# A two-layer hybrid trunk: four low parts of weights made by GpSimd, other banks for one memory attention, two slots for a small state, and a new order

## The chip, the cores and the metric

The kernel runs on one core of a Trainium2 chip. A core has engines that run side by side, each with its own queue of instructions: TensorE (PE in the profile) for matmuls, VectorE (DVE), ScalarE (ACT), GpSimd (POOL), and SyncE (SP), which issues the transfers from HBM to SBUF. Every queue is worked off in order. The metric is the device time of one execution in microseconds (us). Three runs of the kernel before took 1055.48, 1057.3 and 1059.38 us, so the median is 1057.3.

## The reference

Two layers over 256 tokens of width 1024, each of them three residual steps with a layer norm:

```python
for i in range(DEPTH):
    x = layer_norm(ALPHA * x + 0.5 * swiglu(x, ffn1_w_gate[i], ffn1_w_up[i], ffn1_w_down[i]), ln_g[i, 0], ln_b[i, 0])
    if i % N_MIXERS == 0:
        proj = x @ rwkv_w_in[j]
        mix = rwkv7_mix(proj[..., :RWKV_SHIFT], ...)
        mq = proj[..., RWKV_SHIFT:]
    else:
        proj = x @ sb_w_in[j]
        mix = stick_breaking_mix(proj[..., :c], proj[..., c:2 * c], proj[..., 2 * c:3 * c])
        mq = proj[..., 3 * c:]
    heads = jnp.concatenate([mix, memory_attention(mq, mem_k, mem_v)], axis=-1)
    x = layer_norm(ALPHA * x + heads @ w_out[i], ln_g[i, 1], ln_b[i, 1])
    x = layer_norm(ALPHA * x + 0.5 * swiglu(x, ffn2_w_gate[i], ffn2_w_up[i], ffn2_w_down[i]), ln_g[i, 2], ln_b[i, 2])
```

`swiglu` is `(silu(x @ w_gate) * (x @ w_up)) @ w_down` with an inner width of 2816. `rwkv7_mix` is a delta-rule recurrence over 12 heads of 64; its decay, its gate and its learning rate come from a low-rank part of the projection. `memory_attention` is a softmax attention of 4 heads over 256 memory tokens. All weights are float32 and are used once: some 300 MB are read from HBM.

## The kernel before

**Precision.** A product of float32 accuracy is made from three matmuls on rounded operands (type float32r): high part of the weight times high part of the activation, low times high, high times low (`mm3`, L858). So each weight is loaded in pieces of 128 x 1024 (512 KB) into a `raw` buffer; ScalarE copies it, rounded, into a `hi` buffer; VectorE subtracts the two and writes the rest to a `lo` buffer. That is `piece` (L824 to L846). There are 11 raw, 9 hi and 8 lo buffers, which are used in turn. A raw buffer is free for the next load when its low part has been made. For some chunks of the FFNs (the table `WHOLE`) w_down is used in plain float32, straight from the raw buffer.

**Stages.** The 256 tokens are two halves of 128. The FFN's inner width is cut into 11 chunks of 256: gate and up into PSUM banks of the tag `gu` (two banks), SiLU and product on ScalarE and VectorE, then the down product into the accumulators `acc0` (half 0) and `acc1` (half 1), two banks each; a fourth tag, `tp`, holds two banks for transposes and small work. While one half goes through the mixer (`rwkv`, L1213, in layer 0, `stick`, L1688, in layer 1), whose chains of small steps leave TensorE idle, chunks of the other half's FFN are mixed into it. In layer 0 `memory_kv` makes the keys and values of the memory, and `mem_attention(0, ..., MEMTAG)` (L1118, called at L1889) attends for half 0 near the end of that half's recurrence; MEMTAG names the tag of its banks. `mixed_out` multiplies by w_out; it takes the four row blocks of w_out in the sequence of a tuple in `ORDERS`, which it gets by number: 0 or 1 for half 0 (the layer), 3 for half 1. In `rwkv` the low-rank state `zl` has one buffer for both halves (L1259).

**What sets the order.** The program is recorded first and ordered afterwards. Class `Plan` (L296) records each instruction; `order` (L516) places them engine by engine, with a price for each operation (`price`, L457), and picks among the ready ones by priority; `improve` (L723) takes the priorities from the table `URGENCY`, a packed list of one number for each instruction, and the same numbers set the sequence in which loads, high parts and low parts go through their buffers. `issue` then emits all of them from one line, so nearly every instruction of the profile is at L788. In the names of the trace hi_49r or raw_15r is a buffer, not a weight.

Of the kernel before, what the change touches and what calls it, by code (L numbers as in the profile page):

```python
# [133 lines left out]
CHUNK0 = 94.7  # L134
ROUNDS = 50
# [8 lines left out]
    '+ZY#j58=v>V*I{r2%is%@tbQy7@-!goQW}iC9yi^DCd8%d<fS%%T3nVF2)sp3RDlFlCxc2G=z(<3L$ri5OVg7@f~qiliM4fjxn29N)-wr|H&A0T6'
    'e`maxIS!Hwodn4QjbQ#z&tCVaAuP^ZZn2*f%+ZLXXDy+vpIAf2Iz8w@~+D;;1Nw=-RPzxaF-F8~+sJyy+nfNQw8|7!URg;W0T~>8uxOsntX3Cy%+'
    'lk8y;!a@BF})9_R}#yQW&c%+8&zYXhm!%poG%J+zIbgvLPu2=f)F~0Cvj9+~i<6o^pxLfUOIM4TEVyq^A1=RA3>q59r9_wA33I!I*iSxX4PYA^d+'
    'wbmFsO{cdex8G+*{5SXaf@DZO`!+Hup-7iax?FS5WdV2W6|9q{AKN1+J}(6jI-FIhd#J5BO?@8k~`e>>YwrM3aPNOcskBcrT<SK6nid&()wc4Jux'
    'ml7Q)}lVti21n>B|MxNqc4kHX8579lLZS^n#VFkNj6sl`s`IaAHKPNd^2rBmVXzj8iMzF@lL+8B4~rTZI(Q2ogeIt+{PX8<mx*1y~z<LhnU4^FRX'
    'DZcz6xGc1mkN<v)u|%5~v&iuSS=2mxD*UQncER@eIWbO3$5_krH%<wm@_f1d2WA(9(0>TLT5}8>9~uzCp*Lb2G&qET{oNz>#baaKB7dtEIm2IK7#'
    '`zn*Z*)+jO*rwaI@!MUn3s5p3)rN9<g^<^{%d7W98nujel0#M!0C2{#CO9^1fBR#;t{!zti#D+i(Z7<3EqF^cx|dfcS&6uDw1LhMZ5w?)v>hn6Kb'  # L150
    '$-S?;COn90zTTN%B!tEE*@mGCx6Py-Q-%?+OFcGfmi=&FT#<UKhOScfF>Vt7JV;m`;ch?MIkep?mV$W;TXj2Fe&VtGPF}{qS3c~YfoHSgWs=g-wZ'
    '^7Ro_u_=Yui{>Lx+QBWZ2u!2d+Mvn_<NP}UDFQ+#6L;Sc2y1GQ#F6OMU3l<!@70vJC%-CKB}h9-&;R*EdhJhDsTV7xbS6!aqK(seGtM-N%&;4T09'
    'oQ{K_FL?4n0&$JnBGD&$`i;|#qr?|n7;i8lO|j`v(CrVsSXeXcDSLR<B?AcpdAGZQCGfd8w+T0^h2uN%Vme$Ny0P3~>|JFKZu3D<1KJ0Gjx2bZVg'
    'A9}OGarin8BOR^PEQE5MV;nNqHH}lDuo{-b7ro&ji#{DQFdh5;7D5v>p3y%Q=H3-!Q*q^8mX6zZ(WZ7G%!2O{a<TIzJmlV_*SpY^=k(meUfT&zv-'
    ';sPI=Esr9MFemU#Vxy5T2?Z!dcj@lkmR&>@mZ>8F&j%O~ogm61zLsr}}aVT)q7b{N)H?Bd+|g2_C+HSMlU1{Cz@gf2TS3;MF}-L%4jN`oewDYhr9'
    'Gwtg^QOOM<RFB|uzW1~G8Ve|*-SXYnFnPgwQw@IJg>h-E>)T>pDZ^`42@X=^pjQ{*Egs*Y)KxZu@)^_T(N*&(&I>!G-dAuitcm7Mq9l28B**v&Q4'
    '^&pGtn{bTelbr>$BcL6`{NMqxWrnkLwL7wI<8o(xBf>9^!A>LFh`Hp*|WQTObwUwg7S-tf02_s;wubOEk^Jat7v^T{joX5;>&R;JpU<<ulm3vt^b'
    '*3w<-xEH|d{RF^-XwT&rkIkq}PPuKn-DxWQ|CXw52|T8Iw4qNh&E?>2o=QS6r_7}C4V9uV*07)$#5o-bnTrj~nQex|%1_IEM$UaF?^)b>{W*HUfD'
    'rS&z_Fnj?nv`>52Wx@GF^y~pV*vEb|JomYp?S;!?F!_k{T|=XDKN#a-d8#>5&0zWoxzB*pEIsrBeteBbDbX<<*Yg6)pGbw>xaKSSEpCz#E|#~3*3'
    'I`%2;1|fV|F#nhcDW?r{rK7h<gu+^96je<TY9?-nVv$uNd4~@AYl+DYjnn(s5smH{1WhuQ7Ip#fE&?MDg9PM(=p8jh>(C_a}ZXJc85Q_Y`jaPhaG'  # L160
    'w1=U_mg+2{jcWsQvXW>}+y_0A7-0RD6$jh*n8^;!q*VXiEt{V2%UmIv_S3aUV>}+;zSDtSGY-GhtO=<9Peq@?hZ-(_6xbz1(IjI&^X!yJQz%KezQ'
    'QzOxAQj%9o{rrTznS2w0zTRv!YKE5mxJT-^aee-4vtsBbYA<vej|TkuZQ@DM59J~?ppfypBT=l&*AgxmuQc33>W89uvk)GU%54ePFvIQWqSM#4PA'
    'qC>frdp@LCdnYg=P7++QVEd7Lq8Ovfj0OodbWdp7>=Xa7d{Y6wkT!=t_FT;=HJ&Gf5)ntdqVoUW<u9F3cX@G7p{fLqr(%k$QqQaFT)@b#1WUGM(u'
# [1763 lines left out]
```

## Time and profile before

| what | value |
|---|---|
| median of three runs | 1057.3 us (1055.48 to 1059.38) |
| the profiled execution | 1058.2 us |
| its span | 1056.4 us |
| mean granted clock of TensorE | 0.995 |
| read from HBM | 300.95 MB, 286 GB/s over the span |

The page gives each engine's busy time and its share of the span. A table by stages gives the busy time of each engine in a stretch, so that a stall in one stage isn't lost in the average. The granted clock is the share of TensorE's full speed that the chip allowed; at 0.50 a matmul takes twice as long. In rows of single instructions the first number is the start, the second the duration; what stands in brackets at the end is the engine's idle time before it and what ended it.

### The profile page before, as it was taken

How to read it: one execution, taken by the hardware profiler on the slowest of the kernel's cores; microseconds unless marked ns; L12 is line 12 of the kernel's file. 1: busy time of each engine (PE TensorE's matmuls, PEld its weight loads, DVE VectorE, ACT ScalarE, POOL GpSimd, SP SyncE). 2: the span in 40 equal slices, each digit the busy share in tenths (PEclk: the TensorE clock that was granted, in tenths of full speed). 3: DMA queues.
4: the chain of work that ended last, by engine and by line, in shares of the span. 5: the costliest groups of instructions: out<-in, count | busy, mean ns of one | idle time of the engine just before them, and what ended most of it. 6: DMA issues, size and time to landing. Idle time of an engine off the chain costs nothing.

```text
span 1056.4 us, 17846 instructions
## 1 busy us (share of the span) xinstructions
PE 1041.8 (99%) x6275; PEld 835.8 (79%) x6275; DVE 886.2 (84%) x1241; ACT 741.6 (70%) x1064; POOL 5.3 (0%) x20
## 2 busy tenths in 40 slices
PE   8999999999899999999999999999999999999997
PEld 7788888877788776688888888888778777888885
DVE  6776679999799998898799765569899999976688
ACT  6665558968679877667577555457987998765573
POOL 0000000000000000000000000000000000000000
PEclk9999999999899999999999999999999999999999
DMA  9998869879399788799999976768989989998792
GB/s 307 332 368 259 265 201 357 266 247 331 130 328 336 250 273 295 247 341 315 307 325 352 311 246 208 226 213 262 369 309 315 366 274 304 366 366 256 265 317 76
DMA packets 212684, 303.19 MB, mean 287 GB/s; under 512 B 13892, under 2 KB 159728, under 8 KB 212594
## 3 DMA queue, kind: packets, MB, share of 16 engines
q1 hardware_dynamic: 212050, 301.53, 85.2%
q8 instruction: 49, 0.80, 0.3%
q10 hardware_dynamic: 544, 0.52, 0.2%
q14 instruction: 41, 0.34, 0.1%
HBM read 300.95 MB, written 1.05 MB: 286 GB/s over the span
## 4 chain that ended last, share of the span: by engine, by line
PE 95%; DMA 2%; DVE 1%; ACT 1%; issue 0%; SPq 0%; DVEq 0%; ACTq 0%
PE ps_30r L788 28%; PE ps_29r L788 27%; PE ps_26r L788 8%; PE ps_3r L788 8%; PE ps_27r L788 8%; PE ps_25r L788 8%; PE ps_5r L788 3%; PE ps_6r L788 3%; DMA raw_9r<-in_ffn_w_down_dram 1%; DMA raw_18r<-in_ffn_w_up_dram 1%; DMA raw_48r<-in_ffn_w_up_dram 1%; DMA raw_12r<-in_ffn_w_up_dram 1%; DVE x L788 0%; DVE L_345r L788 0%; DVE lo_47r L788 0%
## 5 line engine op out<-in xcount | busy, mean ns | idle before, releaser
L788 PE MATMUL ps_30r<-hi_46r,xTh 128*128 128x512 f32 (+1 forms) x70 | 28.2, 403 | 0.0
L788 PE MATMUL ps_30r<-hi_46r,xTl 128*128 128x512 f32 (+1 forms) x70 | 26.9, 385 | 0.0
L788 PE MATMUL ps_30r<-lo_17r,xTh 128*128 128x512 f32 x68 | 26.5, 390 | 0.0
L788 PE MATMUL ps_29r<-lo_11r,xTh 128*128 128x512 f32 (+1 forms) x64 | 24.6, 385 | 0.8 <-DVE lo_11r L788 0.8
L788 PE MATMUL ps_30r<-lo_11r,xTh 128*128 128x512 f32 x64 | 25.0, 390 | 0.0
L788 PE MATMUL ps_30r<-hi_10r,xTh 128*128 128x512 f32 x60 | 24.5, 409 | 0.0
L788 PE MATMUL ps_30r<-lo_8r,xTh 128*128 128x512 f32 x62 | 24.2, 391 | 0.0
L788 PE MATMUL ps_30r<-hi_10r,xTl 128*128 128x512 f32 x60 | 23.5, 392 | 0.0
L788 PE MATMUL ps_30r<-lo_14r,xTh 128*128 128x512 f32 x60 | 23.4, 390 | 0.0
L788 PE MATMUL ps_29r<-hi_65r,xTh 128*128 128x512 f32 x56 | 22.8, 407 | 0.0
L788 PE MATMUL ps_29r<-lo_17r,xTh 128*128 128x512 f32 x58 | 22.6, 390 | 0.0
L788 PE MATMUL ps_29r<-lo_47r,xTh 128*128 128x512 f32 (+1 forms) x58 | 22.2, 383 | 0.0
L788 ACT ACTIVATE idle_2r<-ps_29r 128x256 f32<-128x256 f32 (+1 forms) x27 | 11.1, 412 | 15.8 <-PE ps_29r L788 15.2
L788 PE MATMUL ps_30r<-hi_7r,xTh 128*128 128x512 f32 (+1 forms) x56 | 21.9, 392 | 0.0
L788 PE MATMUL ps_29r<-hi_65r,xTl 128*128 128x512 f32 x56 | 21.9, 392 | 0.0
L788 ACT ACT_TABLE_LOAD x16 | 20.5, 1283 | 2.0 <-issue 1.7
L788 PE MATMUL ps_30r<-lo_41r,xTh 128*128 128x512 f32 x56 | 21.9, 390 | 0.0
L788 PE MATMUL ps_29r<-lo_14r,xTh 128*128 128x512 f32 x56 | 21.8, 390 | 0.0
L788 ACT ACTIVATE idle_1r<-ps_29r 128x256 f32<-128x256 f32 (+1 forms) x27 | 11.7, 432 | 14.3 <-PE ps_29r L788 14.3
L788 PE MATMUL ps_30r<-hi_7r,xTl 128*128 128x512 f32 (+1 forms) x56 | 21.4, 383 | 0.0
L788 PE MATMUL ps_30r<-hi_65r,xTh 128*128 128x512 f32 x52 | 21.4, 412 | 0.0
L788 ACT ACTIVATE idle_2r<-ps_30r 128x256 f32<-128x256 f32 (+1 forms) x30 | 12.9, 431 | 12.0 <-PE ps_30r L788 12.0
(2124 smaller groups left out, 3945.5 us busy)
## 6 DMA issues: line engine op xcount, KB each, us to landing
raw_9r<-in_ffn_w_down_dram SPq DMA_DIRECT2D x16, 512.0 KB, 6.7
raw_48r<-in_ffn_w_down_dram SPq DMA_DIRECT2D x16, 512.0 KB, 6.0
raw_12r<-in_ffn_w_down_dram SPq DMA_DIRECT2D x16, 512.0 KB, 6.2
raw_18r<-in_ffn_w_gate_dram SPq DMA_DIRECT2D x31, 256.0 KB, 5.0
raw_18r<-in_ffn_w_up_dram SPq DMA_DIRECT2D x31, 256.0 KB, 4.6
raw_15r<-in_ffn_w_down_dram SPq DMA_DIRECT2D x15, 512.0 KB, 5.8
raw_9r<-in_ffn_w_gate_dram SPq DMA_DIRECT2D x30, 256.0 KB, 5.9
raw_9r<-in_ffn_w_up_dram SPq DMA_DIRECT2D x30, 256.0 KB, 5.8
```

Source lines behind the costliest of these rows:

```text
L788: fn(*[at(x) for x in a], **{n: at(x) for n, x in k.items()})
```

## The change

Four things change, and with them the order of the whole program.

1. `POOLED` names four low parts; `piece` has GpSimd do the subtraction for these, and VectorE for all others as before.
2. `MEMTAG` is 'gu' instead of 'acc1': memory attention for half 0 of layer 0 uses the two banks of gate and up.
3. `FLAGS["zl2"]` is on: `zl` has two buffers, one for each half.
4. The third tuple of `ORDERS` is another, and `URGENCY` is a new table.

```diff
-MEMTAG = 'acc1'
+MEMTAG = 'gu'
...
-ORDERS = ((3, 1, 2, 0), (1, 0, 2, 3), (2, 0, 3, 1), (3, 0, 1, 2))
-FLAGS = dict(t1=False, bt=False, dc=False, out1=False, zl2=False, pb=False, xt=False, mn=False, tn=False, vn=False, sq=True)
+ORDERS = ((3, 1, 2, 0), (1, 0, 2, 3), (1, 0, 2, 3), (3, 0, 1, 2))
+FLAGS = dict(t1=False, bt=False, dc=False, out1=False, zl2=True, pb=False, xt=False, mn=False, tn=False, vn=False, sq=True)
...
+POOLED = ('lo_882', 'lo_977', 'lo_1793', 'lo_1834')
...
-    'c-l?edAN<`8#exXZJ`Vel1617LVQJ~5}C>rqRb-7EK`I`Wr$LSMCK;Slp#|pG*IS>qJdB(A{9}r`}cX?{X35L{bL_{ueF}%zOVbb&g(qSYpq4?jW'
...
+    '3gd$uY'
...
-            made.append(nc.vector.tensor_sub(lo[:, part], raw[:, part], hi[:, part].bitcast(F32)))
+            by = nc.gpsimd if lo.tensor.name in POOLED else nc.vector
+            made.append(by.tensor_sub(lo[:, part], raw[:, part], hi[:, part].bitcast(F32)))
```

TensorE has the same 5261 matmul instructions in both programs; on average a group of them stands three places from where it stood. Three places are shown.

GpSimd, from the last memset of Y (the second half's recurrence in layer 0) to the end. Before:

```order
L788 MEMSET Y_340r 128x32x4
L788 MEMSET Lm_333r 128x768
L788 MEMSET Lm_333r 128x12x16
L1923 UNCONDITIONAL_BRANCH
L1923 ISA
```

and with the change, where `ISA` in the second row is a reload of GpSimd's library, put there in front of its first arithmetic, and raw, hi and lo are a piece's three buffers:

```order
L792 MEMSET Y_340r 128x32x4
L792 ISA
L792 TENSOR_TENSOR lo_17r<-raw_15r,hi_7r 128x1024
L792 MEMSET Lm_333r 128x768
L792 MEMSET Lm_333r 128x12x16
L792 TENSOR_TENSOR lo_17r<-raw_42r,hi_49r 128x1024
L792 TENSOR_TENSOR lo_41r<-raw_42r,hi_62r 128x1024
L792 TENSOR_TENSOR lo_17r<-raw_42r,hi_49r 128x1024
L1928 UNCONDITIONAL_BRANCH
L1928 ISA
```

The first subtraction came in between the memset of Y and that of Lm, the other three behind. The pieces are one of ffn2_w_down and one of ffn2's gate and up in layer 0, one of w_out and one of sb_w_in in layer 1.

SyncE, the loads of gate and up in FFN 2 of layer 0 that come next after that first piece (each raw buffer takes one load of gate and one of up). Before, at place 276 of its queue:

```order
L788 DMA raw_67r<-in_ffn_w_gate_dram 128x2x256
L788 DMA raw_67r<-in_ffn_w_up_dram 128x2x256
L788 DMA raw_70r<-in_ffn_w_gate_dram 128x2x256
L788 DMA raw_70r<-in_ffn_w_up_dram 128x2x256
L788 DMA raw_64r<-in_ffn_w_gate_dram 128x2x256
L788 DMA raw_48r<-in_ffn_w_gate_dram 128x2x256
L788 DMA raw_18r<-in_ffn_w_gate_dram 128x2x256
```

and at the same place with the change, with ScalarE's high parts of these loads behind them:

```order
L792 DMA raw_93r<-in_ffn_w_gate_dram 128x2x256
L792 DMA raw_93r<-in_ffn_w_up_dram 128x2x256
L792 DMA raw_15r<-in_ffn_w_gate_dram 128x2x256
L792 DMA raw_15r<-in_ffn_w_up_dram 128x2x256
L792 DMA raw_9r<-in_ffn_w_gate_dram 128x2x256
L792 DMA raw_18r<-in_ffn_w_gate_dram 128x2x256
L792 DMA raw_64r<-in_ffn_w_gate_dram 128x2x256
L792 ACTIVATE hi_62r<-raw_15r 128x1024
L792 ACTIVATE hi_10r<-raw_9r 128x1024
L792 ACTIVATE hT_487r<-ps_5r 128x512
L792 ACTIVATE eT_611r<-ps_6r 128x512
L792 ACTIVATE hi_13r<-raw_18r 128x1024
```

The third and fourth loads go into raw_15r now, the buffer that GpSimd's first subtraction reads, and so wait for GpSimd. (hT and eT are the turned softmax tiles of half 1's memory attention.) The hi_13r of the last row is read by TensorE in the pair `ps_29r<-hi_13r,xTh` and `ps_29r<-lo_41r,xTh`, at places 1584 and 1585 of its queue; at 1585 and 1586 it had `ps_29r<-hi_13r,xTh` and `ps_29r<-lo_14r,xTh` before.

TensorE, the scores of half 0's memory attention in layer 0, between two groups of the recurrence (vn, Sk; S, qr). Before:

```order
L788 MATMUL ps_26r<-vn_314r,Sk_344r 64x64 x2
L788 MATMUL ps_25r<-vn_314r,Sk_344r 64x64 x2
L788 MATMUL ps_27r<-memKT,mq_331r 128x256
L788 MATMUL ps_3r<-memKT,mq_331r 128x256
L788 MATMUL ps_6r<-S_113r,qr_377r 64x64 x2
L788 MATMUL ps_5r<-S_113r,qr_377r 64x64 x2
```

and with the change:

```order
L792 MATMUL ps_25r<-vn_314r,Sk_344r 64x64 x2
L792 MATMUL ps_26r<-vn_314r,Sk_344r 64x64 x2
L792 MATMUL ps_30r<-memKT,mq_331r 128x256
L792 MATMUL ps_29r<-memKT,mq_331r 128x256
L792 MATMUL ps_5r<-S_113r,qr_377r 64x64 x2
L792 MATMUL ps_6r<-S_113r,qr_377r 64x64 x2
```

Both stand at places 1193 to 1200 of TensorE's queue; the banks moved (ps_27r and ps_3r to ps_30r and ps_29r, and ps_25r, ps_26r and ps_5r, ps_6r traded places), the sequence did not.

More of the change, by code (lines that the diff above doesn't have):

```diff
@@ L144 @@
[L144 to L163, printed above, removed]
@@ new lines @@
+    'RB4LiOk9`Qt^dq8xN6Z->5+Yk?Jc_)@$S1L7!B;se$!#4c4{ypK5ttuR_gM^4hDGB5yxaqn)NMC?XO+S;S$4>Y7?24X>*XeJfJ1jq2TN)Y4gG8@;'
+    'H{p6k~X`E^dUr=LjP_o}|sECXvxWUWu;imYe9HQR`+8!NJ_uWIGLs(!vAvpKHsdDVsmMFOv=7RX9%&eF3Cs+A^){A2HvrikQvW@>rrKk~V1+w39}'
+    '8dIw{)rAM?V>^+ecUS|jPh?%)Gl}>-ruO|roH_r^G9n9E|Lk$9_lL3udUbSzYD?;Ho;{aLP2X?Q_aP~@9XeCwJ$>+BtJ;CSeB=DhIlfpYkyPElL?'
+    '5mhDiZrd)!r1Wonmi3eBVK&CAC;VU9T+`@gA-^F^eIOqD<WztUA1{h$H*lrXpnmRKGL_$E>?QI2pJU9MHqz=L~7oRyFvVsXJZ4-Wt{as6lSdoxD)'
+    '>c}GJgA5mSriGGBb+VrgIoZ=#<2GTp~?#6X?o)OuyUo}5__D`pp_nskpJXCvAXR{CIN;I`zDMQM@gVbQ;#8B`7c6zesaqFq^0gjDU?OcamE>W$rU'
@@ new lines @@
+    '3G+;A?bWX+)UMSKBk@-CbAj)eQ~f!?-3bgSh-~NHw?+_ZEE(5cAfE=bF37p%9>`)RJ~V#zQc=E98)Tz>Xu-U;_T;gNv^?rJ=sS)u$u~Oxt^pSJw&'
+    '>mP|Z?6wND8{2D7gloO2u)q3qgiFW5RR@`bwJqKCt_zz;Zcth4I)*&?4OimdIgnw9=kL_6*;5IJ{Mwe$dRdtanMR%%Hff|gRt(S~^3Hucq0)&TAr'
+    '7ZNGN=YD@sz3N0=U#nKnDbj8OytuDAHHXNPIPiDR)bKeXd#F!Q)|ECMzHOriwM8=D5b3j7H4J_w+*Msx&yeWUVCWNkZl}5d{%-wd>irKQEo#G+qa'
+    'xYUiLA(D$l9Bx&IYqSRaLL^`n@iylb*uyIjZTvzso$4W~WtOftQ8bM8bNgexe3_z)Rs>hRoS)*Ura8+N-IpUx?K1D&hx5kGrU*MpN$6yMzFd{OCy'
+    '@@OS3ANZY(<L36Z_wYC6Hzr0mxuV#evpLVg{d*BoO)R(IJzpHvs$HLpu2Q)1Z{66;-X>t)PvTkQrxJ7RQxW+s`)womeqNr-qNg_$;;$gUv6s9^Yg'
@@ L291 @@
+    'm+8B`7`j<U_3D$^?JI&)CA_0tLW4Ra!#*L<Oe)2<3Y5!C0KDIYl6)U+rbMS7Xs$z6jmKD%hX%wX43OivIE_2LjC@cw+~mKCy|DfMT1^@+2k@B|9='
+    '3gd$uY'
 )
```

274 lines of the change are left out of this document (143 added, 131 removed).

## The prediction

> **What bounds the kernel now.** I read the page first: the busy shares and the chain that ended last.
>
> ```profile
> PE 1041.8 (99%) x6275; PEld 835.8 (79%) x6275; DVE 886.2 (84%) x1241; ACT 741.6 (70%) x1064; POOL 5.3 (0%) x20
> PE 95%; DMA 2%; DVE 1%; ACT 1%; issue 0%; SPq 0%; DVEq 0%; ACTq 0%
> ```
>
> TensorE is busy for 1041.8 of the 1056.4 us of the span and carries 95% of the chain. A change that leaves its matmuls alone can take at most 1056.4 − 1041.8 = 14.6 us, plus what a slow clock makes the busy time longer. So the second view is a table by stage: where TensorE is idle, and where its clock drops.
>
> ```profile
> 268.00:272.00 4.00, 3.47 (x136) 2.84 (x139) 2.90 (x7) 2.16 (x5) 0.00 (x0) 1.00 0.95 347
> 272.00:276.00 4.00, 2.00 (x57) 1.54 (x50) 3.49 (x8) 2.96 (x10) 0.67 (x3) 0.84 0.04 14
> 276.00:280.00 4.00, 3.77 (x100) 3.25 (x100) 1.27 (x4) 3.11 (x8) 0.00 (x0) 0.50 0.01 4
> 280.00:282.00 2.00, 1.58 (x9) 1.45 (x10) 1.90 (x6) 0.63 (x2) 0.00 (x0) 0.62 0.53 143
> 420.00:440.00 20.00, 19.43 (x181) 12.79 (x181) 17.20 (x33) 10.65 (x16) 0.00 (x0) 1.00 0.65 209
> 1048.50:1056.40 7.90, 0.00 (x0) 0.00 (x0) 4.83 (x14) 0.20 (x1) 0.00 (x0) 0.78 0.19 66
> ```
>
> In each row the length comes first, then busy time of PE, weight loads, DVE, ACT and POOL; the third number from the end is the granted clock. The last 7.9 us have no matmul at all: the last layer norm and the stores. Between 268 and 282 TensorE idles 0.53 + 2.00 + 0.23 + 0.42 = 3.2 us, and after the 2.00 us its clock is at 0.50. The three granted clocks 0.84, 0.50 and 0.62 amount to 0.16 × 4 + 0.50 × 4 + 0.38 × 2 = 3.4 us of lost clock, some 3 of them while there was work. This stall, where the delta-rule state of half 0 and the memory attention of half 0 meet, is worth 3.2 + 3 = about 6 us. The third view, what TensorE waited for, shows that little else is left:
>
> ```profile
> PE ps_6r L788 <- DVE L_345r L788: 1.8, 2, 1.2
> PE ps_29r L788 <- DVE lo_11r L788: 0.8, 1, 0.8
> PE ps_5r L788 <- DVE S_113r L788: 0.6, 1, 0.6
> PE ps_6r L788 <- ACT memKT L788: 0.5, 1, 0.5
> PE ps_26r L788 <- DVE lo_50r L788: 0.2, 1, 0.2
> ```
>
> Only two short waits in the whole run are for a low part of a weight (lo_11r at the start, lo_50r). VectorE is late with a low part nowhere else, even where it is nearly full:
>
> ```profile
> 320.00:340.00 20.00, 20.00 (x116) 17.19 (x116) 19.69 (x31) 19.89 (x39) 0.00 (x0) 1.00 1.04 353
> 780.00:800.00 20.00, 20.00 (x96) 14.33 (x95) 19.68 (x34) 14.47 (x20) 0.00 (x0) 1.00 0.84 277
> 800.00:820.00 20.00, 20.00 (x97) 16.63 (x96) 19.83 (x32) 15.73 (x19) 0.00 (x0) 1.00 0.93 323
> ```
>
> VectorE has 19.7 of 20 us there, TensorE 20.00 of 20. A lighter VectorE in these windows buys no time.
>
> **The change part by part.** The sum is made against the profiled execution: 1058.2 us, 1.8 us of it outside its span of 1056.4. The median of the runs shown is 1057.3, 0.9 lower.
>
> *Memory attention in the gate and up banks.* The scores and outputs of half 0 go to ps_30r and ps_29r instead of ps_27r and ps_3r. Around the stall the rows of TensorE, VectorE and ScalarE stand in the same sequence as before, only with banks and buffers swapped. The waits named above come from data (L_345r, S_113r, memKT), not from a bank of the memory attention. The gate and up matmuls that take the banks next stood behind it on TensorE already. Cost 0; if a bank were the cover, the gate of the next chunk could be held back by the output's last eviction, some 0.6 us.
>
> *Two slots for the low-rank state.* Half 1 could write its state before half 0 had read its own. Before, the tile's second writing began long after the first state's last use:
>
> ```profile
> L788 ACT ACTIVATE zl_315r<-ps_5r,vc x4: 352/364/368, 171.3 to 313.3; 128x128 f32<-128x128 f32 x4
> 268.12 0.33 PE L788 MATMUL ps_5r<-vn_314r,kn_313r 64*64 64x64 f32 x4
> ```
>
> The last reader of half 0 (the product with g_up) stands just ahead of the matmuls at 268.12, and half 1's last writing starts at 313.3. More than 40 us lie between. Cost 0.
>
> *The third tuple of ORDERS.* Half 0 uses the first two, half 1 the fourth; the third is read by no one. Cost 0.
>
> *The new order.* TensorE issues the same matmuls with as many changes of shape; most rows move by a few places. It can win back the small waits outside the stall: 0.57 us in 420 to 440, 0.2 for lo_50r, and as much again elsewhere, 1 to 2 us; it can lose as much. I take −0.5.
>
> *Four low parts on GpSimd.* Removed from VectorE are four subtractions, 4 × 1.22 = 4.9 us, in stages where it has slack enough for TensorE:
>
> ```profile
> 345.74 1.22 DVE L788 TENSOR_TENSOR lo_44r<-raw_67r,hi_10r 128x1024 fp32r<-128x1024 f32 x1
> 384.57 0.74 POOL L788 MEMSET Lm_333r<- 128x768 f32 x1 [38.73 <-PE ps_6r L788]
> 345.63 0.21 POOL L788 MEMSET Y_340r<- 128x128 f32 x1 [69.75 <-DVE RB_336r L788]
> L788 ACT ACT_TABLE_LOAD x16 | 20.5, 1283 | 2.0 <-issue 1.7
> raw_9r<-in_ffn_w_down_dram SPq DMA_DIRECT2D x16, 512.0 KB, 6.7
> ```
>
> GpSimd did no arithmetic before. From below such a subtraction takes VectorE's 1.22 us. From above, the memset of 768 elements took 0.74 us, so one pass over 1024 is 0.99, and two reads and a write as three separate passes are 3.0 us. I take two passes, 2.0 us. By the Trainium skill (GPSIMD Engine Reference, section 3.1) a two-input operation of 2048 elements takes 4.5 us there, by estimate 2.25 for 1024; nothing below changes by this 0.25.
>
> Ahead of the first of them the changed order has an extra instruction on GpSimd, a reload of its library. No row of before shows one. The nearest load of code or tables is ScalarE's, 1.28 us; the other end is what fetches 512 KB, 6.7 us. I take 1.3. Now the places, from the order of the changed kernel and the times of before:
>
> 1. lo_17r from raw_15r (FFN 2's w_down, layer 0). GpSimd first makes the memset of Y, which ended at 345.84, then the reload, then the subtraction, so it ends at 345.84 + 1.3 + 2.0 = 349.1. TensorE needs this lo only with that chunk's down product, over 10 us later. But SyncE's next load, gate and up into raw_15r, waits for GpSimd, and all loads are queued behind it. In the row of the same place before, that load went out at 351.59:
>
> ```profile
> 351.59 0.37 SPq L788 DMA_DIRECT2D raw_70r<-in_ffn_w_gate_dram  x1
> 357.39 1.04 ACT L788 ACTIVATE hi_46r<-raw_70r 128x1024 fp32r<-128x1024 f32 x1
> 361.63 0.59 ACT L788 ACTIVATE hT_487r<-ps_6r 128x512 f32<-128x512 f32 x1
> 363.57 0.40 PE L788 MATMUL ps_29r<-hi_13r,xTh 128*128 128x512 f32 x1
> 363.81 0.39 PE L788 MATMUL ps_29r<-lo_14r,xTh 128*128 128x512 f32 x1
> ```
>
>    From issue to the high part's start took 5.8 us (351.59 to 357.39). In the changed order ScalarE makes this high part, a second, two turned softmax tiles and the third high part (1.04 + 1.04 + 0.59 + 0.59 + 1.04 = 4.3), then VectorE its low part (1.22), all for the pair of matmuls that stands where 363.57 and 363.81 stand. 363.81 − 5.8 − 4.3 − 1.2 = 352.5, and 0.5 for the hand-overs: GpSimd must be done by 352.0. At 349.1 there are 2.9 us to spare. Cost 0, as long as the reload stays under 4.2 us.
> 2. to 4. (lo_17r and lo_41r from raw_42r, for layer 0's FFN 2, layer 1's w_out and sb_w_in.) Here the cover is TensorE's other work between the release of the low part's buffer, or of its high part, and its use, at these paces:
>
> ```profile
> 71.05 5.45 PE ps_29r L788 x24
> 352.50 1.02 PE L788 MATMUL ps_25r<-raw_48r,eT_611r 128*128 128x512 f32 x2
> 353.35 1.02 PE L788 MATMUL ps_25r<-raw_18r,hT_487r 128*128 128x512 f32 x2
> ```
>
>    5.45 / 24 = 0.227 us for a matmul with rounded weights, 353.35 − 352.50 = 0.85 for one with plain weights. The changed order has 25 and 6 of them in the first of these places (10.8 us, besides 200 small ones), 14 and 4 in the second (6.6), 38 and 0 in the third (8.6). A subtraction of 2.0 us, and 1.04 for the high part where it comes first, leave 4 us and more. SyncE's next load into raw_42r waits as well; in the tightest place, the second, its high part is due 27 and 4 matmuls after the release: 9.5 − 2.0 − 5.8 leaves 1.7 us. Cost 0; at 3.0 us a subtraction still 0.
>
> Sum: 1058.2 − 0.5 = 1057.7 on the profiled basis, 1056.8 for the median. I say 1057.0.
>
> A rule that speaks against the change: by the Trainium skill (SBUF — State Buffer, section on who interferes with whom) a VectorE instruction with two inputs in SBUF and a GpSimd instruction that reads SBUF share a port, and the later one blocks for the whole of the other. VectorE's low parts are such instructions. By the rule each GpSimd subtraction could hold VectorE for its own 2.0 us, which turns a gain of 1.22 into a loss of 0.8, four times; no run shown here lets one see it.
>
> **The rivals.**
>
> *Slower, by the library reload.* The reload takes as long as a fetch, 6.7 us. Then raw_15r comes free at 345.84 + 6.7 + 2.0 = 354.5, 2.5 us after 352.0, with the whole load queue behind it. TensorE waits 2.5 us around 364, and as in 272 to 276 (2.00 us busy of 4.00) its clock falls for a while, the 3.4 us of above. 2.5 + 3.4 = 5.9: 1062.7. It decides from 4.2 us on; from 6.1 with the lower clock it is beyond the bound of 0.5%. Against it: the instruction waits for nothing and could be short where nothing has to be loaded. By the Trainium skill (GPSIMD Engine Reference, section 2.1) the first call of a freshly loaded kernel pays about 6 us, unseen in the profile; by estimate that makes 345.84 + 5.95 + 2.25 = 354.0 and 2.0 us lost before any change of clock.
>
> *Slower, by VectorE.* Each subtraction on GpSimd holds VectorE up by its own length. At 780 to 820, where VectorE has 0.2 to 0.3 us free in 20, two times up to 3.0 − 1.22 = 1.8 us push later low parts back; 3.6 us exposed and a fall of the clock by 3.4 give 1064. Against it: no low part is waited for there now.
>
> *Faster, by the stall.* The searched order starts a part of the chain at 268 to 282 earlier, the idle time falls under what drops the clock, and 5 to 6 of the 6 us go: 1051. For it: this is the one place worth the whole bound. Against it: the sequence on three engines is the same there.
>
> *Nothing happens.* All parts lie off the path and the order neither wins nor loses: 1057.3, inside my forecast.
>
> **How the numbers follow.** This kernel's measurement tells about 0.5%, 5.3 us, from no change. Forecast with the last rival 0.57; reload 0.18; VectorE and other late loads 0.10; stall gone or the small waits with part of it 0.15. So faster 0.15, same 0.57, slower 0.28. The forecast's own range is 1054 to 1060 (±2 for the order, 2 more for a reload of about 6 us). The range for 8 in 10 goes down to 1050, past the stall's 1051, and up to 1065, past 1062.7 and 1064.
>
> **What would show it.** Right: four TENSOR_TENSOR rows on POOL of about 2 us, the first by 350; no wait of TensorE for a lo or hi between 355 and 375; the clock at 0.50 once, after 274; PE at about 1041 of a span near 1055.5. Wrong: a gap on POOL ahead of its first subtraction of over 4 us, a load into raw_15r issued after 352 and a second stretch at half clock (reload); VectorE rows of 128x1024 longer than 1.3 us beside POOL's (the port); the windows 272 to 282 at full clock (stall gone). A POOL row of over 3 us would break the bound on which places 2 to 4 rest.

## The result

The changed kernel takes 1065.14 us (median of 4 runs, 1064.74 to 1065.63) against 1056.91 us for the kernel before on the same chip (4 runs, 1055.48 to 1059.38). The ratio is 1.0074, with a 95% interval of 1.0062 to 1.0087: 6.6 to 9.2 us slower. The prediction said 1057.0, in 1050 to 1065. The profiled execution has a span of 1063.3 us (before: 1056.4) and a mean granted clock of 0.997 (before: 0.995), so the clock is not where the time went.

The page of the changed kernel, busy shares and chain:

```profile
PE 1042.3 (98%) x6275; PEld 835.0 (79%) x6275; DVE 889.7 (84%) x1239; ACT 742.4 (70%) x1062; POOL 16.5 (2%) x24
PE 90%; DMA 4%; DVE 4%; ACT 1%; issue 1%; SPq 0%; DVEq 0%; ACTq 0%
```

TensorE is busy about as long as before (1041.8). Of the 6.9 us by which the span grew, 6.4 are new idle time: 1063.3 − 1042.3 = 21.0 against 14.6. Its share of the chain falls from 95% to 90%. What TensorE waited for in the changed kernel (engine and tile, total us, times, longest; a selection, like the list in the prediction):

```profile
PE ps_3r L792 <- DVE rn_380r L792: 1.7, 1, 1.7
PE ps_6r L792 <- DVE x L792: 1.6, 1, 1.6
PE ps_5r L792 <- DVE L_345r L792: 1.2, 1, 1.2
PE ps_3r L792 <- ACT Sk_344r L792: 1.1, 1, 1.1
PE ps_6r L792 <- ACT Lm_333r L792: 0.9, 1, 0.9
PE ps_5r L792 <- ACT bn_384r L792: 0.7, 1, 0.7
```

Before, the long waits were L_345r, lo_11r, S_113r and memKT, which are still there, and Lm_333r with 0.6 us. New are rn_380r and x, both by VectorE, Sk_344r and bn_384r by ScalarE, and 0.6 us for the low part lo_41r at 28 us. Both kernels also wait 1.0 us for lastc near the start, which neither list shows. The table by stages tells where they lie (columns as in the prediction):

```profile
272.00:276.00 4.00, 2.60 (x78) 1.85 (x74) 3.68 (x8) 2.07 (x7) 0.20 (x1) 1.00 0.22 83
276.00:280.00 4.00, 3.09 (x100) 2.76 (x100) 1.92 (x6) 3.76 (x11) 0.63 (x2) 0.73 0.01 4
340.00:360.00 20.00, 18.33 (x124) 12.16 (x123) 19.60 (x44) 15.33 (x34) 3.38 (x2) 1.00 0.53 161
420.00:440.00 20.00, 19.42 (x227) 12.88 (x226) 16.64 (x33) 11.69 (x17) 0.00 (x0) 1.00 0.73 242
800.00:820.00 20.00, 18.39 (x86) 14.97 (x85) 19.76 (x27) 13.65 (x17) 2.04 (x1) 1.00 0.84 272
820.00:840.00 20.00, 19.31 (x112) 15.24 (x110) 19.82 (x25) 18.08 (x26) 0.00 (x0) 1.00 1.08 366
880.00:900.00 20.00, 18.87 (x120) 15.47 (x119) 15.64 (x19) 12.43 (x17) 0.00 (x0) 1.00 0.75 244
```

The stall at 272 to 280 is still there, and 420 to 440 has the idle time it had (19.42 against 19.43). But 800 to 820, where TensorE was busy for 20.00 of 20, has lost 1.6 us; 340 to 360 has lost 1.7, 820 to 840 has lost 0.7, 880 to 900 has lost 1.1. Two of these four stretches have GpSimd in them, and two do not.

GpSimd's subtractions (the second, 2.40 us at 401.98, left out), with the memset that stands ahead of the first (start, duration, engine, line; in brackets the idle time before):

```profile
344.57 0.20 POOL L792 MEMSET Y_340r<- 128x128 f32 x1 [67.81 <-ACT vn_314r L792]
344.92 3.18 POOL L792 TENSOR_TENSOR lo_17r<-raw_15r,hi_7r 128x1024 fp32r<-128x1024 f32 x1
...
784.75 2.40 POOL L792 TENSOR_TENSOR lo_41r<-raw_42r,hi_62r 128x1024 fp32r<-128x1024 f32 x1 [380.37 <-PE ps_28r L792]
798.92 3.13 POOL L792 TENSOR_TENSOR lo_17r<-raw_42r,hi_49r 128x1024 fp32r<-128x1024 f32 x1 [11.78 <-PE ps_25r L792]
```

The memset ends at 344.77 and the subtraction starts at 344.92: the library reload between them took 0.15 us at most. A subtraction takes 2.40 us, or 3.1 to 3.2 in the first and the fourth place. Beside these two, VectorE has rows that are far too long:

```profile
344.93 0.95 DVE L792 TENSOR_TENSOR Sk_344r<-kn_313r,L_345r 128x768 f32<-128x768 f32 x1
345.80 2.34 DVE L792 SCALAR_TENSOR_TENSOR rn_380r<-nw_381r,rn_380r 128x12 f32<-128x12 f32 x1
...
799.69 2.38 DVE L792 SCALAR_TENSOR_TENSOR mv_574r<-nw_381r,mv_574r 128x1 f32<-128x1 f32 x1
```

and TensorE waits behind each of them:

```profile
348.19 0.27 PE L792 MATMUL ps_3r<-cst,rn_380r 64*64 64x64 f32 x1 [1.67 <-DVE rn_380r L792]
804.02 0.66 PE L792 MATMUL ps_6r<-cst,x 128*128 128x128 f32 x4 [1.61 <-DVE x L792]
```

In the kernel before, the same one-column step took 0.15 us:

```profile
798.91 0.15 DVE L788 SCALAR_TENSOR_TENSOR mv_574r<-nw_381r,mv_574r 128x1 f32<-128x1 f32 x1
```

Sk_344r is put down 0.01 us after GpSimd's first instruction but ran at its length of before (0.96 us); GpSimd waited for it (3.18 − 2.40 = 0.8). In the fourth place it waited in the same way for a subtraction that VectorE had begun at 798.55. Then GpSimd had its turn, and an operation on 12 columns stood on VectorE for 2.34 us until GpSimd was through. These two places explain 3.3 us of idle time. They do not explain the rest, and what stands idle in a window need not be lost at the end.

### The profile page after: what moved, and what is told of

The parts are those of the page before. It is cut to its first block, busy times and chain, and to the rows that moved or that the text cites. A ratio compares the mean times of both kernels' runs of the same rounds, so it can differ in the third digit from the quotient of the medians.

```text
span 1063.3 us, 17884 instructions
## 1 busy us (share of the span) xinstructions
PE 1042.3 (98%) x6275; PEld 835.0 (79%) x6275; DVE 889.7 (84%) x1239; ACT 742.4 (70%) x1062; POOL 16.5 (2%) x24
## 4 chain that ended last, share of the span: by engine, by line
PE 90%; DMA 4%; DVE 4%; ACT 1%; issue 1%; SPq 0%; DVEq 0%; ACTq 0%
PE ps_30r L792 28%; PE ps_29r L792 25%; PE ps_26r L792 8%; PE ps_3r L792 8%; PE ps_28r L792 8%; PE ps_25r L792 7%; PE ps_5r L792 3%; PE ps_6r L792 3%; DMA raw_70r<-in_ffn_w_gate_dram 1%; DMA raw_12r<-in_ffn_w_up_dram 1%; DMA raw_42r<-in_ffn_w_up_dram 1%; DMA raw_64r<-in_ffn_w_down_dram 1%; DVE x L792 1%; DMA raw_48r<-in_ffn_w_gate_dram 1%; DMA raw_15r<-in_ffn_w_gate_dram 1%
## 5 line engine op out<-in xcount | busy, mean ns | idle before, releaser
L792 PE MATMUL ps_30r<-lo_14r,xTh 128*128 128x512 f32 (+1 forms) x76 | 29.2, 384 | 0.0
L792 PE MATMUL ps_30r<-hi_40r,xTh 128*128 128x512 f32 x64 | 26.1, 408 | 0.0
L792 PE MATMUL ps_30r<-hi_40r,xTl 128*128 128x512 f32 x64 | 25.0, 391 | 0.0
L792 PE MATMUL ps_29r<-hi_40r,xTh 128*128 128x512 f32 x62 | 24.8, 401 | 0.0
L792 PE MATMUL ps_29r<-hi_40r,xTl 128*128 128x512 f32 x62 | 24.2, 391 | 0.0
L792 PE MATMUL ps_29r<-lo_11r,xTh 128*128 128x512 f32 x60 | 23.5, 392 | 0.6 <-DVE lo_11r L792 0.6
L792 PE MATMUL ps_29r<-hi_13r,xTh 128*128 128x512 f32 x58 | 24.1, 415 | 0.0
L792 PE MATMUL ps_30r<-hi_16r,xTh 128*128 128x512 f32 (+1 forms) x60 | 23.4, 391 | 0.0
L792 PE MATMUL ps_30r<-lo_50r,xTh 128*128 128x512 f32 x60 | 23.4, 390 | 0.0
L792 PE MATMUL ps_29r<-hi_13r,xTl 128*128 128x512 f32 x58 | 22.7, 391 | 0.0
```

Of the source, the lines that this page charges most:

```text
L792: fn(*[at(x) for x in a], **{n: at(x) for n, x in k.items()})
```

## The experiments

Two questions: what does GpSimd cost, and what does the order cost by itself? Times are medians; each run's ratio is to runs of the kernel before on the same chip.

### The new order with the subtractions put back on VectorE

Four kernels, each with the change's order on every engine; in `piece` some of the four subtractions are recorded as before (so that the order stays) but issued to VectorE:

```diff
             made.append(by.tensor_sub(lo[:, part], raw[:, part], hi[:, part].bitcast(F32)))
+            if lo.tensor.name in ('lo_882', 'lo_977', 'lo_1793', 'lo_1834'):
+                made[-1].calls = [(nc.real.vector.tensor_sub,) + made[-1].calls[0][1:]]
```

All four, then the first and the fourth (`lo_882`, `lo_1834`), then the first alone, then the fourth alone:

> The changed kernel, its order word for word, with all four low parts made by VectorE again. Theory (a GpSimd subtraction holds VectorE up): the two waits of 1.67 us at 346 and 1.61 us at 802 go, and with them most of the 2.4 us that TensorE lost between 820 and 900, since those began with loads that came late after 802; 1065.1 - 3.3 - 2.4 = 1059.4, and not above 1060.5. Rival (the new order is slower by itself, GpSimd only stands beside it): 1063.5 to 1065.

> Only the two low parts back on VectorE beside whose subtraction on GpSimd VectorE had an instruction of 2.3 us in place of 0.17 (the first and the last); the second and third stay on GpSimd. Theory: the same as with all four back, within 1 us, so about 1059.4. Rival that each of the four costs its share: half of the gain of all four. Rival that the order alone is slower: 1063.5 to 1065.

> Only the first low part (ffn2_w_down, layer 0) back on VectorE. Theory: the wait of 1.67 us at 346 goes and nothing else does: 1063.4. Rival that the order alone is slower: 1065.

> Only the last low part (sb_w_in, layer 1) back on VectorE. Theory: the wait of 1.61 us at 802 goes, and the 2.4 us lost between 820 and 900 with it, if they follow from it: 1061.1; if they belong to the new order, 1063.5. Rival that the order alone is slower: 1065.

| on VectorE again | us | range | ratio to before |
|---|---|---|---|
| none (the change) | 1065.14 | 1064.74 to 1065.63 | 1.0074 [1.0062, 1.0087] |
| first | 1064.48 | 1064.19 to 1064.67 | 1.0066 [1.0053, 1.0078] |
| fourth | 1064.96 | 1062.56 to 1066.32 | 1.0067 [1.0052, 1.0083] |
| first and fourth | 1064.00 | 1062.80 to 1070.53 | 1.0072 [1.0048, 1.0095] |
| all four | 1063.75 | 1062.92 to 1064.26 | 1.0058 [1.0046, 1.0070] |

The theory that GpSimd makes most of the loss fell. With GpSimd out of it altogether 1.4 of 8 us come back, and even that is at the edge of the noise, since the intervals of the first and the last row overlap. The single steps between are too small for these intervals. The idle time beside GpSimd did go: of the kernel with all four on VectorE the windows read

```profile
340.00:360.00 20.00, 19.85 (x132) 13.35 (x132) 19.82 (x46) 16.65 (x34) 0.20 (x1) 1.00 0.62 190
800.00:820.00 20.00, 19.86 (x91) 16.10 (x90) 19.62 (x33) 15.19 (x17) 0.00 (x0) 1.00 0.87 294
```

that is, 1.5 us gained in each. Over the whole span, however, TensorE idles only 2.0 us less (1062.3 − 1043.3 = 19.0 against 21.0): part of what is gained comes back as idle time elsewhere, in this profile 0.5 us at 270 to 290 and 0.3 at 420 to 440. Some 6 us are left to the order.

### Which part of the change, and which part of the order

To put orders together, a list of all instructions in their sequence replaces the table, and `Plan.order` follows it:

```diff
-URGENCY = (
+GIVEN = (
...
-                o = ops[given[done]]
+                o = next((ops[i] for i in pending if not ops[i].left and earliest(ops[i]) is not None), None)
...
-        best = self.order()
+        best = self.order(given)
```

With the list of the kernel before, every engine runs that kernel's rows in that kernel's sequence. The two lists can be cut at a point where they have handled the same instructions, near 800 us of the profile. Three kernels have the change's banks, its two slots and its third tuple, and all subtractions on VectorE: the change's order up to the cut and the old one behind it; the reverse; the old order throughout.

> The changed kernel with all four subtractions on VectorE, cut at the tile that is under way at about 800 us of the profile: on every engine the rows ahead of the cut stand in the changed kernel's order, the rows behind it in the order of the kernel before. The whole new order on VectorE alone gave 1063.75 us, the kernel before 1056.9. Theory (most of the new order's loss lies behind the cut, in the stick chains of the last blocks, where PE lost 3.2 us between 829 and 884 us): 1059.5 to 1061. Rival (the loss is spread over the whole program, or made by the slots of the low-rank state and the banks, which stay): 1062.5 to 1064.

> The other half: the same cut, with the kernel before's order ahead of it and the changed kernel's order behind it, all subtractions on VectorE. Theory: the last quarter alone brings the 3 to 4 us, 1060 to 1061.5. Rival (the loss is made ahead of the cut): 1057 to 1058.5.

> Memory attention in the gate and up banks, the low-rank state in two slots and the third tuple as the change has them, but every engine's instructions in the order of the kernel before, and all subtractions on VectorE. Theory (these three edits cost nothing in themselves; they matter only as what the search started from): 1056.5 to 1058, no change against the kernel before. Rival (a bank or a slot comes free later and holds an accumulation up): 1059 or more.

| order | us | range | ratio to before |
|---|---|---|---|
| old throughout, new banks and slots | 1057.30 | 1055.83 to 1059.85 | 1.0000 [0.9991, 1.0009] |
| new, then old | 1059.47 | 1057.34 to 1061.82 | 1.0020 [1.0010, 1.0030] |
| old, then new | 1061.00 | 1059.99 to 1061.91 | 1.0034 [1.0021, 1.0047] |
| new throughout (the run above) | 1063.75 | 1062.92 to 1064.26 | 1.0058 [1.0046, 1.0070] |

The kernel before had 1057.11 beside the first three. So banks, slots and tuple cost nothing that these runs could see (1 us either way). The new order ahead of the cut costs 2.4 us (1.1 to 3.2 by the interval), behind it 3.9 (2.2 to 5.0); in sum 6.3, and the whole new order costs 1063.75 − 1057.67 = 6.1 beside its own runs of before. The order's loss adds up from places, and by the medians the larger part lies in the last quarter. There the sums of the windows from 800 to 900 us say it plainly; first of the kernel before, then of "new, then old", then of "old, then new":

```profile
sum 100.00, PE 100.00 PEld 79.50 DVE 95.49 ACT 88.96 POOL 0.00; mean PE 20.00 PEld 15.90 DVE 19.10 ACT 17.79 POOL 0.00
```

```profile
sum 100.00, PE 100.00 PEld 79.48 DVE 95.42 ACT 88.92 POOL 0.00; mean PE 20.00 PEld 15.90 DVE 19.08 ACT 17.78 POOL 0.00
```

```profile
sum 100.00, PE 97.45 PEld 76.22 DVE 92.03 ACT 84.72 POOL 0.00; mean PE 19.49 PEld 15.24 DVE 18.41 ACT 16.94 POOL 0.00
```

With the old order TensorE does not idle at all in these 100 us, while VectorE is at 95% and ScalarE at 89%. With the new one it idles 2.55 us.

A single profile can also be timed behind the cut alone. The last matmul that reads eT_1713r (layer 1's memory attention) stands some 25 us ahead of the cut in all these kernels. From its start to that of the program's last matmul, first in the kernel before, then in "old, then new":

```profile
773.57 0.27 PE L788 MATMUL ps_26r<-eT_1713r,memV 128*64 128x128 f32 x1
1048.19 0.28 PE L788 MATMUL ps_30r<-hi_10r,hT_1954r 128*128 128x256 f32 x1
```

```profile
771.82 0.27 PE L695 MATMUL ps_26r<-eT_1713r,memV 128*64 128x128 f32 x1
1050.44 0.28 PE L695 MATMUL ps_29r<-hi_46r,hT_2024r 128*128 128x256 f32 x1
```

That is 274.6 us against 278.6: the 4.0 us of the loss behind the cut, free of what the profiles differ by ahead of it. The old order with the new banks takes 274.6 too, "new, then old" 275.0.

Ahead of the cut the loss is spread over several small places. These two windows of "new, then old" read 10.00 and 20.00 on TensorE in the old order throughout; the first holds the wait for lo_41r:

```profile
20.00:30.00 10.00, 9.27 (x42) 7.36 (x41) 6.26 (x7) 5.61 (x8) 0.00 (x0) 1.00 1.08 318
240.00:260.00 20.00, 19.48 (x251) 14.46 (x253) 19.32 (x37) 17.29 (x32) 0.26 (x1) 1.00 0.96 334
```

Which of the two it is changes from one profile to the next: in the six kernels with the new order ahead of the cut TensorE idles for 0.2 to 1.3 us in the two together, in the ten with the old order for 0.02 at most. Where the rest of the 2.4 us lies was not tested.

### GpSimd in the old order

The kernel before, untouched, with the same four subtractions issued to GpSimd; then with only the first three there; then with all four, the fourth cut into four instructions of 256 columns.

```diff
+            if lo.tensor.name in ('lo_882', 'lo_977', 'lo_1793', 'lo_1834'):
+                made[-1].calls = [(nc.real.gpsimd.tensor_sub,) + made[-1].calls[0][1:]]
+            if lo.tensor.name == 'lo_1834':
+                made[-1].calls = [(nc.real.gpsimd.tensor_sub, (lo[:, j:j + 256], raw[:, j:j + 256], hi[:, j:j + 256].bitcast(F32)), {})
+                                  for j in range(0, D, 256)]
```

> The kernel before in its own order on every engine, with the subtractions of the same four names moved to GpSimd and nothing else. Theory (GpSimd costs 1.3 us on the new order because two of the four subtractions hold a VectorE operation that PE waits for; in the old order other operations stand beside them): 1057 to 1060, so 0 to 2.5 us above the kernel before, with VectorE rows of two SBUF inputs stretched to 2 us and more beside the GpSimd rows. Rival (VectorE, with 1.2 us less to do at each place, gains): 1055 to 1056.5.

> The kernel before with only the first three of those subtractions on GpSimd, the fourth on VectorE as it was. Theory (the fourth alone costs: it is the only place of that order where PE waits behind a stretched VectorE row, 1.7 us): 1057 to 1058, no change against the kernel before. Rival (each of the four costs some tenths wherever it stands): 1058.5 to 1059.5.

> The kernel before with the same four subtractions on GpSimd as in the last experiment of that order (1059.6 us), the fourth of them cut into four instructions of 256 columns. Theory (one GpSimd instruction keeps VectorE's operations of two SBUF inputs out for as long as it runs, 2.40 us here, so a quarter keeps them out for a quarter): the one-column VectorE row near 798 us takes 0.6 to 0.8 us in place of 2.36, PE's wait for x falls from 1.7 to 1.0 or less, 1058 to 1059. Rival (VectorE is kept out until GpSimd's whole queue of such work is done, or each slice costs as much again): the wait stays or grows, 1059.5 to 1061.

| on GpSimd | us | range | ratio to before |
|---|---|---|---|
| all four | 1059.61 | 1058.92 to 1060.92 | 1.0024 [1.0015, 1.0033] |
| first three | 1057.48 | 1057.00 to 1058.34 | 1.0005 [0.9997, 1.0014] |
| all four, the fourth in quarters | 1059.23 | 1057.63 to 1062.01 | 1.0024 [1.0014, 1.0033] |

Without the fourth nothing is left that these runs can tell from no change; by the medians it alone makes 2 of the 2.5 us. Rows of the kernel with all four there, VectorE at the first place, then VectorE and TensorE at the fourth:

```profile
344.29 0.16 DVE L788 SCALAR_TENSOR_TENSOR rn_380r<-nw_381r,rn_380r 128x12 f32<-128x12 f32 x1
797.75 2.36 DVE L788 SCALAR_TENSOR_TENSOR mv_574r<-nw_381r,mv_574r 128x1 f32<-128x1 f32 x1
801.40 0.66 PE L788 MATMUL ps_5r<-cst,x 128*128 128x128 f32 x4 [1.69 <-DVE x L788]
```

In the first place rn_380r ran at 344.29, just before GpSimd began at 344.60, and took 0.16 us. In the new order it came 0.9 us behind GpSimd's start and took 2.34. Which of the four hurts depends on which small operation happens to come behind it. In quarters, at the fourth place:

```profile
799.25 4.08 POOL L788 TENSOR_TENSOR lo_44r<-raw_48r,hi_7r 128x256 fp32r<-128x256 f32 x4 [13.75 <-PE ps_25r L788]
801.26 0.69 DVE L788 SCALAR_TENSOR_TENSOR mv_574r<-nw_381r,mv_574r 128x1 f32<-128x1 f32 x1
801.99 0.67 DVE L788 SCALAR_TENSOR_TENSOR nw_381r<-mv_574r 128x1 f32<-128x1 f32 x1
```

The step takes 0.69 us in place of 2.36: VectorE is kept out for one instruction of GpSimd, as the theory had it. But four one-column steps in a row, from 799.51 to 802.69, now wait for a quarter each (0.65 to 0.70 us), and TensorE's wait for x falls only from 1.7 to 1.4 us, not to 1.0. The time did not move by what can be told. The lock was read rightly, the gain from cutting it up was not.

### Behind the cut: VectorE or TensorE's own order?

What the new order changed at 872 to 880: TensorE in the kernel before, from the last step of the stick chain (the product with Y) on. The rows that read Sk_344r begin the two groups of products that need the chain's result; between them stands other work, of which one row is shown:

```profile
874.04 0.34 PE L788 MATMUL ps_6r<-Y_1927r,tri_1871r 128*128 128x384 f32 x1
...
875.22 0.44 PE L788 MATMUL ps_3r<-Sk_344r,gup_111r 128*64 128x128 f32 x4
...
876.68 1.12 PE L788 MATMUL ps_26r<-raw_45r,eT_1924r 128*128 128x512 f32 x2
...
879.12 0.44 PE L788 MATMUL ps_3r<-Sk_344r,gup_111r 128*64 128x128 f32 x4
```

and in "old, then new":

```profile
875.77 0.34 PE L695 MATMUL ps_6r<-Y_1927r,tri_1871r 128*128 128x384 f32 x1
876.04 0.44 PE L695 MATMUL ps_3r<-Sk_344r,gup_111r 128*64 128x128 f32 x4
...
877.40 0.38 PE L695 MATMUL ps_27r<-Sk_344r,gup_111r 128*64 128x128 f32 x2
878.91 0.32 PE L695 MATMUL ps_27r<-Sk_344r,gup_111r 128*64 128x128 f32 x1 [1.13 <-ACT Sk_344r L695]
```

In the old order 1.2 us pass from the start of the chain's last step to the first products (874.04 to 875.22), filled with matmuls on weights, and 2.4 us of such work (876.68 to 879.12) stand between the first group and the second. In the new one it is 0.3 us (875.77 to 876.04), nothing stands between the groups, and the second one, begun at 877.40, waits 1.13 us for an Sk that goes from TensorE through VectorE and ScalarE. VectorE is late with it as well: between two of the chain's steps it has two subtractions in a row, and its last step on Sk (877.75) stands right behind a third (876.62). In "old, then new":

```profile
869.59 0.55 DVE L695 TENSOR_TENSOR Sk_344r<-Sk_344r,ps_5r 128x384 f32<-128x384 f32 x1
...
870.52 1.22 DVE L695 TENSOR_TENSOR lo_11r<-raw_48r,hi_40r 128x1024 fp32r<-128x1024 f32 x1
871.66 1.22 DVE L695 TENSOR_TENSOR lo_44r<-raw_64r,hi_43r 128x1024 fp32r<-128x1024 f32 x1
```

In the kernel before one stands there, with the chain's next step at 870.12:

```profile
868.98 1.22 DVE L788 TENSOR_TENSOR lo_41r<-raw_51r,hi_13r 128x1024 fp32r<-128x1024 f32 x1
```

Four kernels part the two. Eight subtractions that stand there are computed for a quarter of their columns only, and the rest of these low parts is left out, in "old, then new" and, as a control, in the old order throughout:

```diff
+            if lo.tensor.name in ('lo_2010', 'lo_2013', 'lo_2016', 'lo_2019', 'lo_2029', 'lo_2032', 'lo_2035', 'lo_2038'):
+                made[-1].calls = [(nc.real.vector.tensor_sub, (lo[:, :256], raw[:, :256], hi[:, :256].bitcast(F32)), {})]
```

> Old order ahead of the cut at about 800 us, new order behind it (1061.0 us), with eight low-part subtractions that stand between the stick chain's steps at 859 to 877 us computed for 256 of their 1024 columns; the rest of those low parts is left out. VectorE has some 6.5 us less to do there; every order stays. Theory (VectorE is full in this stretch and the new order lets two and three subtractions stand between two steps of the chain, so that ScalarE's Sk and then PE come late): the waits for Sk and qr, 1.5 us, and the slower stretch beside them go, 1058.5 to 1060; the wait for bn at 825 us stays. Rival (PE waits there for ScalarE, which is full too, or by its own order): 1060.5 to 1061.5.

> The control: the same eight subtractions at 256 columns (the rest of those low parts left out) in the old order throughout, 1057.3 us with them whole. Theory (PE waits for nothing there in the old order, so VectorE's spare time buys nothing): 1056.5 to 1058. Rival (the shorter work helps by itself, through memory traffic or the clock): 1054 to 1056.

Then TensorE's order alone, with whole subtractions, and both together. The rows of TensorE that moved (the other product rows and the bank's later users change their bank only):

```diff
+MATMUL ps_27r<-hi_13r,xTh 128x512
+MATMUL ps_27r<-lo_17r,xTh 128x512
+MATMUL ps_27r<-hi_13r,xTl 128x512
...
 MATMUL <-Sk_344r,gup_111r and <-qr_377r,vn_314r, the second group
...
-MATMUL ps_3r<-hi_13r,xTh 128x512
-MATMUL ps_3r<-lo_17r,xTh 128x512
-MATMUL ps_3r<-hi_13r,xTl 128x512
```

> Old order ahead of the cut, new order behind it (1061.0 us), and on TensorE six matmuls of the next projection (hi_13r and lo_17r, 1.4 us at 0.227) moved from behind the second group of the last stick products to ahead of it; nothing else moves, the product group and the projection trade banks. Theory (half of the loss is TensorE's own order: nothing stands between the chain's last step and the products that need it): PE's wait for Sk falls from 1.1 to 0.3 or less, 1060 to 1060.5. Rival (lo_17r or the traded bank is as late as Sk was): the wait goes to them, 1061 to 1061.5.

> The same six matmuls moved, and the eight subtractions between the chain's steps computed for 256 of their 1024 columns as in the run that gave 1060.2 us (the rest of those low parts is left out). Theory (VectorE's lateness and TensorE's order together make the loss between 860 and 900): waits for qr and Sk under 0.3 in sum, PE busy for 39.5 of the 40 us, 1059 to 1060; what is left above the old order's 1057.3 stands at 820 to 860. Rival (the chain is late by ScalarE): the wait for Sk stays at 0.8, 1060 to 1061.

| kernel | us | range | PE idle, 800 to 900 us | waits for qr and Sk | eT_1713r to last matmul |
|---|---|---|---|---|---|
| old, then new | 1061.00 | 1059.99 to 1061.91 | 2.55 | 0.4 and 1.1 | 278.6 |
| with eight short subtractions | 1060.24 | 1059.00 to 1062.73 | 1.86 | none and 0.8 | 277.7 |
| with six matmuls moved | 1060.56 | 1060.17 to 1062.35 | 1.62 | 0.3 and none | 278.2 |
| with both | 1060.14 | 1058.80 to 1063.49 | 1.29 | none and none | 277.6 |
| old order, eight short | 1056.81 | 1055.79 to 1057.57 | 0.00 | none and none | 274.6 |

The waits answer as the theory has it: a lighter VectorE takes away the wait for qr and a part of that for Sk, TensorE's own order the whole of that for Sk, both together both. The control gains nothing (ratio 1.0001, 0.9992 to 1.0010): where TensorE waits for nothing, a lighter VectorE is worth nothing. The times of the runs follow by 0.4 to 0.9 us only, less than their ranges can settle, and all three lie just above what the theory gave (1060.24 for 1058.5 to 1060; 1060.56 for 1060 to 1060.5; 1060.14 for 1059 to 1060). The last lies inside its rival's 1060 to 1061 as well, but the wait for Sk on which that rival rests is gone. The stretch behind eT_1713r shows the gain more sharply: 0.9 us with the short subtractions, 0.5 with the matmuls moved, 1.0 with both. In the kernel with both, TensorE's longest waits between 780 and 900 us are 0.7 us for bn_384r and 0.2 for xTh, both by ScalarE, the first in a place that no edit touched, the second behind the moved bank.

So where are the 4.0 us of "old, then new"? Six waits make the 2.55 us of idle time, and each is counted some 0.17 us too short. A row counts as busy to its modelled end, but in an unbroken series the next matmul starts earlier than that: the row at 877.40 ends at 877.78, while such matmuls start every 0.1 us, so that the one at 878.91 would have started at 877.6. With 6 × 0.17 = 1.0 us the six waits come to 3.6 of the 4.0. The two on the chain at 860 to 880 make 0.35 + 1.13 + 0.34 = 1.8, bn_384r at 825 makes 0.7 + 0.17, the other three 0.9 together. Of these only the two on the chain were tested. Taking them away gave back 1.0 us and not 1.8: a new wait for xTh takes 0.4 of it, and the other 0.4 was not traced.

No version of these beats the kernel before. The best that compute the whole result are the old order with the new banks and the kernel before with three subtractions on GpSimd, both of which measure as no change.

## Why the prediction was wrong

**The step that failed** is "The new order": that it can win back 1 to 2 us of small waits, "it can lose as much. I take −0.5". It measured +6.1. The bound on the loss was set by symmetry, from what there was to gain, and that is the error. The loss isn't bounded by the old idle time. From 800 to 900 us the old order had TensorE busy for 100.00 of 100 us with VectorE at 95%: nothing could be won there, and whatever moved could only uncover something. Full TensorE alone is not enough for a loss: from 600 to 800 us and from 900 to 1045 TensorE was as full in the old order, VectorE at 74% and 81%, and there the new order idles for 0.2 us at most. The prediction looked at where the change's own edits stood, and quoted 780 to 820 as a place where "a lighter VectorE buys no time", but did not ask what the many small moves behind it would do to the chain at 860 to 880. "Most rows move by a few places" was taken as harmless; with six matmuls put between the two groups of products, a wait of 1.1 us was gone. What the runs showed in place of −0.5 is a sum of small waits, 3.6 us of them between 800 and 900 us; the 2.4 us ahead of the cut stay open in the main.

**The subtractions** were set at 2.0 us and took 2.40; that alone changes nothing. "Cost 0" for places 1 to 4 was wrong for the fourth in both orders, and for the first in the new one, where TensorE waited 1.7 us behind it. They were judged by who waits for the low part and by the load queue, and both judgements held: raw_15r's next load went out in time (limit 352.0), and TensorE waits for nothing from 350 to 380.

```profile
350.31 0.42 SPq L792 DMA_DIRECT2D raw_15r<-in_ffn_w_gate_dram  x1
```

What was missed is the neighbour on VectorE. The rule was named, and its mechanism is what the rows show: by the Trainium skill (SBUF — State Buffer, section on who interferes with whom) a two-input operation of VectorE from SBUF and a GpSimd instruction that reads SBUF exclude each other for the whole of an instruction, whoever is first. The trace agrees on both sides: 0.16 to 2.34 us for VectorE, 2.40 to 3.18 for GpSimd. The prediction put this into a rival of 0.10 and let it delay low parts. The lock delays whichever operation with both inputs in SBUF comes next, here steps of 12 columns and of one on which TensorE waits. Its exposed time was of the rival's size (1.7 and 1.6 us of waits, for two times up to 1.8); at the end it was worth some 1.4 us in the new order, not clear of the noise, and 2.5 (1.6 to 3.5) in the old. The fall of the clock that the rival added did not come (0.997 over the execution). That this rival's total, 1064, lies near the measured 1065.14 is chance, since most of the loss is the order's. Two signs of being wrong that the prediction named did come, a VectorE row of 128x1024 over 1.3 us (1.52) and GpSimd rows over 3 us (3.18 and 3.13); both point at the lesser part of the loss, and no sign was named for the order.

**The library reload** was set at 1.3 us, between 1.28 and 6.7, and took 0.15 at most; the rival with 0.18 did not come about. By the Trainium skill (GPSIMD Engine Reference, section 2.1) the first call of a freshly loaded kernel costs about 6 us; no row here shows it.

**Banks, slots, third tuple**: 0 each, and no change measured for the three together (1.0000, 0.9991 to 1.0009). The argument from the order of rows around the stall and from the 40 us between the two uses held.

**The stall** at 272 to 282 stayed, as forecast, but the 3 us of lost clock in its price of 6 were read too high (see the last section). The chance of 0.57 for no change rested on all of this, and one term of it, off by 6.6 us, decided.

## What to carry to other kernels

A new order of the whole program is an edit to every stage, not a side effect: read the windows where the bound engine is at 100% and its feeders above 90%, for there this new order had nothing to win, and look at what stands between a chain's last step and the matmul that needs it. Work moved from VectorE to GpSimd is paid for, in these runs, by the next VectorE operation with both inputs in SBUF, however small; place it where that operation is one nobody waits for, or leave it. Change the order and the engine of an instruction in separate runs: together they hid that most of the loss was the order's. And time a stretch between two matmuls that stand in both kernels, besides adding up idle time, which counted each of these waits 0.17 us short.

## What the runs showed that was not expected

The clock's answer to the same stall differs from execution to execution. Up to 800 us the kernel before, "old, then new" and the old order with the new banks have the same sequence on every engine, banks apart, and TensorE idles 2.65 to 2.86 us over 270 to 290 us; but the granted clock there was 0.83, 1.00 and 0.91 in this order of kernels:

```profile
270.00:290.00 20.00, 17.35 (x275) 14.54 (x265) 16.20 (x39) 12.55 (x27) 0.67 (x3) 0.83 0.17 56
```

```profile
270.00:290.00 20.00, 17.18 (x250) 14.09 (x249) 17.91 (x40) 14.27 (x28) 0.67 (x3) 1.00 0.27 83
```

```profile
270.00:290.00 20.00, 17.14 (x280) 14.29 (x273) 17.20 (x41) 13.33 (x28) 0.67 (x3) 0.91 0.21 64
```

Over the ten kernels with this order ahead of the cut it was 0.74 to 1.00, seven times 0.91. The product of lost clock and length, 0.17 × 20 = 3.4 us, overstates what it costs, presumably because part of the slow clock falls on idle time: from the first product of vn_314r and Sk_344r to the first matmul that reads x behind the stall, the three profiles take 49.0 (260.55 to 309.57), 47.2 (259.90 to 307.06) and 48.1 us (260.58 to 308.71). So the prediction's 3 us of clock are about 2, measured against the profile at full clock. They are one draw from a range, and a difference of 2 us between two profiles in this stage says nothing about their order.

VectorE's operations with an input in PSUM ran beside a GpSimd subtraction at the length they have elsewhere (0.87 us for two of 128x256 in the kernel before): at 784.65, while GpSimd ran from 784.75 to 787.15,

```profile
784.65 0.87 DVE L792 SCALAR_TENSOR_TENSOR idle_2r<-idle_2r,ps_30r 128x256 f32<-128x256 f32 x2
...
786.70 1.52 DVE L792 TENSOR_TENSOR lo_14r<-raw_48r,hi_43r 128x1024 fp32r<-128x1024 f32 x1
```

and only the subtraction with both inputs in SBUF, which came 0.45 us before GpSimd's end, was longer than its 1.22 us. No operation that TensorE waits for was held up at the third place, which fits with its costing nothing.
